# A fused attention and SwiGLU block: 14 of its 22 gate/up products by one level of Strassen's scheme

## The chip, the core and the metric

The kernel runs on one core of a Trainium2 chip. That core has a matrix engine (TensorE, PE in the profile; its weight loads are a row of their own, PEld), a vector engine (VectorE, DVE), a scalar engine (ScalarE, ACT), GpSimd (POOL) and a synchronization engine (SyncE, SP) that issues most of the transfers; 16 DMA engines carry them. The metric is the time of one execution on the device, in microseconds, and of several executions the median.

## The reference

One layer of a hybrid block on 512 tokens of width 1024, in float32. Two kinds of attention are followed by a gated merge, an output projection and a SwiGLU feed-forward layer of width 2816 (22 × 128):

```
x  = x + (sigmoid(h Wg_A) * (o_A Wb_A) + sigmoid(h Wg_B) * (o_B Wb_B)) @ W_out
h2 = rmsnorm(x, g_ffn)
ff = silu(h2 @ W_gate) * (h2 @ W_up)          # 1024 -> 2816, twice
x  = x + ff @ W_down                          # 2816 -> 1024
```

Only the second half, from the output projection on, differs between the two kernels in what is computed where.

## The kernel before

Activations lie transposed: 128 features on the partitions, 512 tokens in the columns. A float32 product is made of three passes over fp32r operands. Every operand is split into a high part (a cast on ScalarE, line 86) and a low part, operand minus high part (a subtraction on VectorE, line 87), and `mm3` (lines 204 to 206) issues high × high, high weight × low activation, low weight × high activation into one PSUM bank:

```
nc.tensor.matmul(out=ps, lhsT=wh, rhs=ah, start=first, stop=False)
nc.tensor.matmul(out=ps, lhsT=wh, rhs=al, start=False, stop=False)
nc.tensor.matmul(out=ps, lhsT=wl, rhs=ah, start=False, stop=last)
```

Weights come as blocks of 128x1024 float32 (512 KB) through `Stream`: SP loads `AHEAD` = 5 blocks ahead into six buffers (`raw`), and the high and low parts of a block (`wh`, `wl`) are made two blocks ahead of their use, in four buffers. A scheduler puts the instructions of each engine in order by their dependencies and their order in the program.

The stages, in the span of the profiled execution: projections and the first attention to about 193 us, the second attention, interleaved with gate projections, to 320, the merge to 343.5, the output projection to 387.3. There x after the first residual (`x2`, eight tiles) is made, and from it `h2` = x2 × g_ffn as high and low parts (`h2h`, `h2l`); the norm of each token, `r2`, is made on the side and applied to products.

Then follow the 22 gate/up pairs. Pair n computes 128 features of gate (`pg`) and 128 of up (`pu`), each over 8 tiles of h2, so 2 × 8 × 3 = 48 matmuls of 512 columns (lines 204 to 206), every one with its own 128x128 weights. VectorE multiplies each with r2 (lines 726 and 728, tiles `t`), ScalarE applies silu to the first (line 727), GpSimd multiplies the two (line 729), and the product is split into `fh`, `fl` for the down projection.

The down projection has eight blocks of 22 × 3 matmuls of 512 columns; each ends with one addition of x2 on VectorE (line 740) and a store, the last block in two halves of 256 columns:

```
parts = 2 if d == 7 else 1
for i in range(parts):
    sl = slice(i * S // parts, (i + 1) * S // parts)
    nc.vector.tensor_tensor(out=x2[d][:, sl], in0=ps[:, sl], in1=x2[d][:, sl], op=ALU.add)
```

Far ahead of all this, in the first attention's `qk_norm` (line 300), GpSimd multiplies the normalized q and k (tiles `qn`) with a gain; that is its first work after it has built the identity matrix `ident`.

Of the kernel before, what the change touches and what calls it, by code (L numbers as in the profile page):

```python
# [9 lines left out]
F32 = mybir.dt.float32  # L10
# [5 lines left out]
P = 128  # L16
# [11 lines left out]
N_BLK, N_RAW, N_SPLIT = 66, 6, 4  # L28
DA_ROUNDS, DA_STAGGER, DA_LEAD = 31, 7, 6
SB_ROUNDS, SB_STAGGER = 36, 4  # L30

# [11 lines left out]
def block_kernel(  # L43
# [22 lines left out]
    small = ctx.enter_context(tc.tile_pool(name="small", bufs=4))  # L66
# [27 lines left out]
    class Stream:  # L94
        AHEAD, SPLIT = 5, 2

        def __init__(self, srcs):
            self.srcs, self.raw, self.hl, self.at = srcs, {}, {}, 0

        def load(self, i):  # L100
            if i < len(self.srcs) and i not in self.raw:
                src = self.srcs[i]
                n = src.shape[-1]
                t = wraw.tile([P, 1024], F32, tag="raw", name=f"raw{i}")
                self.raw[i] = (t, n)
                if i >= KT // 2:
                    nc.sync.dma_start(out=t[:, :n], in_=src)
# [22 lines left out]
        def next(self):  # L130
            i = self.at
            self.at += 1
            if i >= KT // 2:
                for j in range(i, i + self.SPLIT):
                    self.split(j)
# [19 lines left out]
    for n in range(NF):  # L155
        srcs += [w_fg[n], w_fu[n]]
    for d in range(8):
        srcs += [w_dn[d, :, 0:1024], w_dn[d, :, 1024:2048], w_dn[d, :, 2048:2816]]

    ws = Stream(srcs)  # L160
# [66 lines left out]
    def proj_ct(ps, acts, first=True, last=True):  # L227
        wh, wl = ws.next()
# [465 lines left out]

    x2, h2 = [], []
    acc = None
    for d in range(8):
# [3 lines left out]
        nc.vector.tensor_tensor(out=xr, in0=ps, in1=xr, op=ALU.add)  # L701
        x2.append(xr)
# [11 lines left out]

    r2 = B(name="r2")
    ff = []
    for n in range(NF):
# [6 lines left out]
        pu = full_ct(h2)  # L724
        t1, t2 = B(name="t1"), B(name="t2")
        nc.vector.tensor_tensor(out=t1, in0=pg, in1=r2, op=ALU.mult)
        nc.scalar.activation(out=t1, in_=t1, func=AF.Silu)
        nc.vector.tensor_tensor(out=t2, in0=pu, in1=r2, op=ALU.mult)  # L728
        nc.gpsimd.tensor_tensor(out=t1, in0=t1, in1=t2, op=ALU.mult)  # L729
        h, l = B(F32R, "fh"), B(F32R, "fl")  # L730
        split(h, l, t1)
        ff.append((h, l))
    for d in range(8):
        ps = full_ct(ff[0:8], last=False)
        full_ct(ff[8:16], ps=ps, first=False, last=False)
        full_ct(ff[16:22], ps=ps, first=False, last=True)
        parts = 2 if d == 7 else 1
        for i in range(parts):
            sl = slice(i * S // parts, (i + 1) * S // parts)
            nc.vector.tensor_tensor(out=x2[d][:, sl], in0=ps[:, sl], in1=x2[d][:, sl], op=ALU.add)  # L740
            (nc.sync, nc.scalar)[i].dma_start(out=out[d * P : (d + 1) * P, sl], in_=x2[d][:, sl])
# [62 lines left out]
```

## Time and profile before

| | |
|---|---|
| three runs | 751.82, 753.04, 753.18 us; median 753.04 |
| profiled execution, span | 751.0 us |
| TensorE matmul busy | 738.1 us, 98%, 3406 matmuls |
| VectorE busy | 431.8 us, 57% |
| ScalarE busy | 325.1 us, 43% |
| GpSimd busy | 103.0 us, 14% |
| DMA | 71.1 MB, mean 95 GB/s |
| gate/up stage | 387.3 to 627.4 us |
| down projection | 627.4 to 747.5 us |

The span is the time from the first to the last thing that the profile of one execution shows; the runs are timed from outside and hold a little more. An engine's busy time is the union of its instructions. The start of a matmul and the start of the next tell what one costs; its own length (390 ns for 512 columns) holds the pipeline's latency and overlaps with its neighbours. "Idle before" in a row is the time that the engine stood still ahead of an instruction, and what is named behind it is what ended that. A row of the windows view names a stretch and its length, then for PE, PEld, DVE, ACT and POOL the busy time with the count of instructions, then the granted clock of TensorE as a share of full speed, the DMA engines' busy share and GB/s. A row of a timeline has start, duration, engine, line, operation, output <- inputs, shapes and count. A row of groups has busy time in all, mean of one in ns, and the idle time ahead.

### The profile page before, as it was taken

How to read it: one execution, taken by the hardware profiler on the slowest of the kernel's cores; microseconds unless marked ns; L12 is line 12 of the kernel's file. 1: busy time of each engine (PE TensorE's matmuls, PEld its weight loads, DVE VectorE, ACT ScalarE, POOL GpSimd, SP SyncE). 2: the span in 40 equal slices, each digit the busy share in tenths (PEclk: the TensorE clock that was granted, in tenths of full speed). 3: DMA queues.
4: the chain of work that ended last, by engine and by line, in shares of the span. 5: the costliest groups of instructions: out<-in, count | busy, mean ns of one | idle time of the engine just before them, and what ended most of it. 6: DMA issues, size and time to landing. Idle time of an engine off the chain costs nothing.

```text
span 751.0 us, 9018 instructions
## 1 busy us (share of the span) xinstructions
PE 738.1 (98%) x3406; PEld 611.6 (81%) x3406; DVE 431.8 (57%) x648; ACT 325.1 (43%) x514; POOL 103.0 (14%) x139
## 2 busy tenths in 40 slices
PE   8999999999989999999999999999999999999998
PEld 6887887888878878888888888888888888888886
DVE  5856877766687887987446454445545533232220
ACT  6633566877566676544444232323232222222110
POOL 0067000000023223300321011101101111000000
PEclk9999999999999999999999999999999999999999
DMA  8622121211121111244432322332232323333200
GB/s 316 218 98 84 59 83 56 81 61 58 57 84 43 46 39 42 73 152 170 161 120 84 113 84 93 105 103 94 85 112 86 98 83 105 103 118 117 64 14 29
DMA packets 23803, 71.12 MB, mean 95 GB/s; under 512 B 2768, under 2 KB 3408, under 8 KB 23760
## 3 DMA queue, kind: packets, MB, share of 16 engines
q1 hardware_dynamic: 23472, 70.40, 28.0%
q8 instruction: 27, 0.44, 0.2%
q10 hardware_dynamic: 288, 0.15, 0.1%
q14 instruction: 16, 0.13, 0.1%
HBM read 68.44 MB, written 2.10 MB: 94 GB/s over the span
## 4 chain that ended last, share of the span: by engine, by line
PE 89%; DVE 3%; POOL 3%; ACT 2%; issue 2%; DMA 0%; DVEq 0%; POOLq 0%; ACTq 0%
PE pc L204 24%; PE pc L205 24%; PE pc L206 24%; PE pt L221 6%; PE pk L221 3%; PE sc L395 1%; PE sc L394 1%; POOL qn L300 1%; DVE wl L87 1%; PE tb L400 1%; ACT wh L86 1%; PE ta L400 1%; PE av L555 1%; POOL qn L314 1%; PE av L556 1%
## 5 line engine op out<-in xcount | busy, mean ns | idle before, releaser
L86 ACT CAST wh<-raw 128x1024 fp32r<-128x1024 f32 (+2 forms) x136 | 130.9, 963 | 299.1 <-PE pc L205 165.4
L87 DVE TENSOR_TENSOR wl<-raw,wh 128x1024 fp32r<-128x1024 f32 (+2 forms) x136 | 172.7, 1270 | 105.3 <-ACT wh L86 101.2
L204 PE MATMUL pc<-h2h,wh 128*128 128x512 f32 x352 | 137.3, 390 | 0.0
L206 PE MATMUL pc<-h2h,wl 128*128 128x512 f32 x352 | 137.0, 389 | 0.0
L205 PE MATMUL pc<-h2l,wh 128*128 128x512 f32 x352 | 136.9, 389 | 0.0
L204 PE MATMUL pc<-hh,wh 128*128 128x512 f32 x192 | 76.6, 399 | 1.9 <-DVE vs L363 1.5
L205 PEld LDWEIGHTS pc<-h2l,wh 128*128 128x128 f32 x352 | 66.1, 188 | 14.1 <-issue 0.2
L204 PEld LDWEIGHTS pc<-h2h,wh 128*128 128x128 f32 x352 | 66.1, 188 | 14.0 <-issue 0.2
L206 PEld LDWEIGHTS pc<-h2h,wl 128*128 128x128 f32 x352 | 66.1, 188 | 13.5
L206 PE MATMUL pc<-hh,wl 128*128 128x512 f32 x192 | 75.5, 393 | 0.0
L205 PE MATMUL pc<-hl,wh 128*128 128x512 f32 x192 | 75.3, 392 | 0.0
L204 PE MATMUL pc<-fh,wh 128*128 128x512 f32 x176 | 68.5, 389 | 0.0
L205 PE MATMUL pc<-fl,wh 128*128 128x512 f32 x176 | 68.5, 389 | 0.0
L206 PE MATMUL pc<-fh,wl 128*128 128x512 f32 x176 | 68.5, 389 | 0.0
L729 POOL TENSOR_TENSOR t<-t,t 128x512 f32<-128x512 f32 x22 | 30.0, 1363 | 208.5 <-DVE t L728 121.0
L728 DVE TENSOR_TENSOR t<-pc,r 128x512 f32<-128x512 f32 x22 | 15.2, 691 | 67.0 <-PE pc L206 63.2
L204 PEld LDWEIGHTS pc<-hh,wh 128*128 128x128 f32 x192 | 36.4, 190 | 9.2 <-issue 1.7
L206 PEld LDWEIGHTS pc<-hh,wl 128*128 128x128 f32 x192 | 36.2, 189 | 7.8
L205 PEld LDWEIGHTS pc<-hl,wh 128*128 128x128 f32 x192 | 36.4, 190 | 6.7
L530 POOL TENSOR_SCALAR_AFFINE_SELECT om<-om 128x128 f32<-128x128 f32 x32 | 11.4, 356 | 210.4 <-DVE obl L87 138.3
L204 PEld LDWEIGHTS pc<-fh,wh 128*128 128x128 f32 x176 | 33.0, 188 | 6.9
L206 PEld LDWEIGHTS pc<-fh,wl 128*128 128x128 f32 x176 | 33.0, 188 | 6.9
(204 smaller groups left out, 1166.4 us busy)
## 6 DMA issues: line engine op xcount, KB each, us to landing
raw<-w_fg_dram SPq DMA_DIRECT2D x22, 512.0 KB, 3.2
raw<-w_fu_dram SPq DMA_DIRECT2D x22, 512.0 KB, 3.2
raw<-w_gate_dram SPq DMA_DIRECT2D x16, 512.0 KB, 3.2
raw<-w_dn_dram SPq DMA_DIRECT2D x16, 512.0 KB, 3.5
raw<-w_tc_dram SPq DMA_DIRECT2D x12, 512.0 KB, 4.5
raw<-w_ct_dram SPq DMA_DIRECT2D x8, 512.0 KB, 3.3
raw<-w_br_dram SPq DMA_DIRECT2D x16, 256.0 KB, 2.6
raw<-w_out_dram SPq DMA_DIRECT2D x8, 512.0 KB, 3.3
```

The costliest lines, as they stand in the source:

```text
L86: a = nc.scalar.copy(out=h, in_=src)
L87: b = nc.vector.tensor_tensor(out=l, in0=src, in1=f(h), op=ALU.subtract)
L204: nc.tensor.matmul(out=ps, lhsT=wh, rhs=ah, start=first, stop=False)
L205: nc.tensor.matmul(out=ps, lhsT=wh, rhs=al, start=False, stop=False)
L206: nc.tensor.matmul(out=ps, lhsT=wl, rhs=ah, start=False, stop=last)
L221: nc.tensor.matmul(out=pss[tb], lhsT=hx[:, tb * P : (tb + 1) * P], rhs=wx[:, wsl], start=(kt == 0 and i == 0), stop=(kt == KT - 1 and i == 2),
L300: nc.gpsimd.tensor_tensor(out=q3, in0=q3, in1=gqkt[:, gi : gi + 1, :].broadcast_to([P, 8, 64]), op=ALU.mult,)
L314: nc.gpsimd.tensor_tensor(out=q3[:, :, 0:16], in0=t1, in1=t2, op=ALU.add)
L400: nc.tensor.transpose(out=ps[:, off + (tb - sb) * P : off + (tb - sb + 1) * P], in_=tiles[tb][:, sb * P : (sb + 1) * P], identity=ident,)
L530: nc.gpsimd.affine_select(out=t[:, o + w - P : o + w], in_=t[:, o + w - P : o + w], pattern=[[-1, P]], compare_op=ALU.is_gt, fill=fill, ba ...
L728: nc.vector.tensor_tensor(out=t2, in0=pu, in1=r2, op=ALU.mult)
L729: nc.gpsimd.tensor_tensor(out=t1, in0=t1, in1=t2, op=ALU.mult)
```

## The change

Of the 22 pairs, 14 (S in `KINDS`) are computed by one level of Strassen's scheme. For such a pair the weights are a 2 × 2 matrix of blocks (gate and up columns, by the lower and upper half of the 1024 inputs), and the activations one of 2 × 2 blocks as well (lower and upper half of the inputs, lower and upper half of the tokens). Seven products of blocks take the place of eight. One product is 4 input tiles × 3 passes = 12 matmuls of 256 columns; a pair has 84. In the form used there are operand sums on both sides.

- Activation sums, `s13` and `s24`, are made once, in plain pairs 1 and 2 (`operand_sums`), from x2 scaled in place by g_ffn. x2 itself is therefore stored to a scratch tensor in DRAM (`x2d`) when it is made, and read back (`xo`) in the down projection.
- Weight sums are made per pair. T1 and T3 (tile `t13`, 128x1024) are two plain loads by SP and one accumulating DMA issued by GpSimd, which adds the third block to both halves. T2 and T4 (`tb2`, `tb4`) are sums on VectorE. x (`rx`), t13, the pair of T2 and T4 (`wlv`, `whv`) and `b21` are each split into a high and a low part: 3.5 blocks of 128x1024, against 2 of a plain pair.
- The seven products (M1, M3, M5, M7, M6, M4, M2 in this order) are combined on VectorE: three operations of 256 columns and two of 512 for gate (`uu`, `t1`) and two of 256 for up (`t2`).
- r2 is applied to gate ahead of silu as before; for up it is left out, and the product of the pair, now on VectorE, is not scaled by it. The output of the down projection is multiplied by r2 instead (`yo`), and the split of the product is made only in the last three plain pairs and ahead of the down projection.
- The plain pairs are 0 to 2, 8, 14 and 19 to 21. From pair 3 on the order on TensorE, VectorE and ScalarE is that of the program text (`manual_schedule`), not the scheduler's. Raw buffers go from six to five, blocks loaded ahead from five to four, `small` buffers from four to three.

```diff
+KINDS = "PPP" + "SSSSSPSSSSSPSSSS" + "PPP"
...
+        def load_t(self):
+            n = self.n
+            self.t13 = tsum.tile([P, 2 * S], F32, tag="t13", name=f"t13_{n}")
+            nc.sync.dma_start(out=self.t13[:, lo_w], in_=w_fu[n, :, lo_w])
+            nc.sync.dma_start(out=self.t13[:, hi_w], in_=w_fg[n, :, hi_w])
+            nc.gpsimd.dma_start(
+                out=self.t13.rearrange("p (a b) -> p a b", b=S),
+                in_=w_fg[n, :, lo_w].unsqueeze(1).broadcast_to([P, 2, S]), accum_op=ALU.add,
+            )
...
+        def sums(self):
+            self.t2, self.t4 = B(name="tb2"), B(name="tb4")
+            tt(self.t2, self.t13[:, lo_w], self.x[:, hi_w])
+            tt(self.t4, self.t2, self.b21)
...
+        def steps(self):
...
+            self.product(6)
+            tt(uu[:, lo_t], m[6], pe[:, lo_t])
+            tt(uu[:, hi_t], m[7], uu[:, lo_t])
+            two = lambda a: a.rearrange("p (a b) -> p a b", b=half)
+            tt(two(self.t1), m[5].unsqueeze(1).broadcast_to([P, 2, half]), two(uu))
+            tt(self.t1[:, lo_t], m[3], self.t1[:, lo_t])
+            tt(self.t1, self.t1, r2, ALU.mult)
+            self.scale = -1.0
+            self.product(4)
+            self.product(2)
...
+        def tail(self):
+            tt(self.t2[:, hi_t], self.m[4], self.uu[:, hi_t])
+            tt(self.t2[:, lo_t], self.m[2], self.pe[:, lo_t])
+
+        def mul(self):
+            tt(self.t1, self.t1, self.t2, ALU.mult)
+            ff.append(self.t1)
...
+        nc.sync.dma_start(out=x2d[d], in_=xr)
...
+    with tc.manual_schedule(engines={ET.PE, ET.DVE, ET.Activation}):
+        for n in range(N_FIRST, NF):
+            call(n + 2, "load")
+            call(n + 3, "load_t")
+            if prev:
+                prev.silu()
+                prev.tail()
+            steps = pairs[n].steps()
+            next(steps)
+            call(n + 1, "low_a")
+            if prev:
+                prev.mul()
+            call(n + 1, "sums")
+            next(steps)
+            call(n + 1, "prep_b")
+            next(steps)
+            call(n + 1, "prep_c")
...
+            next(steps)
+            call(n + 2, "cast_a")
...
+            yo = B(name="yo")
+            nc.vector.tensor_tensor(out=yo[:, sl], in0=ps[:, sl], in1=r2[:, sl], op=ALU.mult)
+            nc.vector.tensor_tensor(out=xr[:, sl], in0=yo[:, sl], in1=xr[:, sl], op=ALU.add)
```

On VectorE a plain pair of before holds five operations: the r2 products of gate and up (L726, L728; their results are t1 and t2), the low parts of two weight blocks (wl) and that of the pair's result (fl). One pair, in mid-stage:

```order
L728 TENSOR_TENSOR t2563_3943<-pc561_3911,r2552_3803 128x512
L87 TENSOR_TENSOR wl71_4026<-raw71_3885,wh71_4025 128x1024
L87 TENSOR_TENSOR fl565_3949<-t1562_3942,fh564_3948 128x512
L726 TENSOR_TENSOR t1568_4014<-pc566_3952,r2552_3803 128x512
L87 TENSOR_TENSOR wl72_4057<-raw72_3916,wh72_4056 128x1024
```

In the changed kernel the same engine holds, in pair 4 with the preparation of pair 5, the low parts of t, b21 and v (wlt, bl, wlv), the evacuation of M6, M7, M5 and M3 (uu, t1), the factor r2, the tail for up (t2), and then the low part of pair 6's x:

```order
L703 TENSOR_TENSOR wlt5_4298<-t13_5_4036,wht5_4297 128x1024
L703 TENSOR_TENSOR bl619_4301<-b21593_4119,bh618_4300 128x512
L703 TENSOR_TENSOR wlv5_4332<-tb2615_4280,whv5_4331 128x512
L703 TENSOR_TENSOR wlv5_4332<-tb4616_4281,whv5_4331 128x512
L703 TENSOR_TENSOR uu612_4274<-pq622_4337,pe611_4273 128x256
L703 TENSOR_TENSOR uu612_4274<-pc621_4318,uu612_4274 128x256
L703 TENSOR_TENSOR t1613_4275<-pc620_4305,uu612_4274 128x512
L703 TENSOR_TENSOR t1613_4275<-pc617_4284,t1613_4275 128x256
L703 TENSOR_TENSOR t1613_4275<-t1613_4275,r2568_3828 128x512
L703 TENSOR_TENSOR t2614_4276<-pq623_4355,uu612_4274 128x256
L703 TENSOR_TENSOR t2614_4276<-pq624_4368,pe611_4273 128x256
L703 TENSOR_TENSOR wlx6_4382<-rx6_4248,whx6_4381 128x1024
```

The pair's product and the two sums T2 and T4 follow. The evacuation stands behind the low parts of v, which wait for ScalarE's casts of T2 and T4.

On TensorE, in the same place, matmuls of 512 columns that all read one accumulating bank (pc584) for eight input tiles stood before:

```order
L204 MATMUL pc584_4168<-h2h524_3591,wh74_4128 128x512
L205 MATMUL pc584_4168<-h2l525_3592,wh74_4128 128x512
L206 MATMUL pc584_4168<-h2h524_3591,wl74_4129 128x512
L204 MATMUL pc584_4168<-h2h529_3632,wh74_4128 128x512
L205 MATMUL pc584_4168<-h2l530_3633,wh74_4128 128x512
```

Now a bank (pc610, M1 of pair 4) takes four input tiles of half the tokens, and M3 follows in another bank (pc617) with the sums s24 as activations:

```order
L207 MATMUL pc610_4260<-h2h529_3637,whx4_4110 128x256
L208 MATMUL pc610_4260<-h2l530_3638,whx4_4110 128x256
L209 MATMUL pc610_4260<-h2h529_3637,wlx4_4111 128x256
L207 MATMUL pc617_4284<-s24h560_3820,whx4_4110 128x256
L208 MATMUL pc617_4284<-s24l561_3821,whx4_4110 128x256
```

The order of these 84 is M1, M3, M5, M7, M6, M4, M2, and ahead of the gate/up pairs TensorE's order is as it was.

On GpSimd, at the program's start, the products of `qk_norm` followed at once behind the identity matrix:

```order
masks.py:199 AFFINE_SELECT ident_121<-ident_121 128x128
L300 TENSOR_TENSOR qn43_342<-qn43_342,gqkt_106 128x512
L306 TENSOR_TENSOR t100_345<-qn43_342,trigt_108 128x128
L310 TENSOR_TENSOR t200_346<-qn43_342,trigt_108 128x8x8 x2
L300 TENSOR_TENSOR qn44_352<-qn44_352,gqkt_106 128x512
```

Now the accumulating DMAs of the first three Strassen pairs stand there; each waits for SP's two plain loads into its t13:

```order
masks.py:199 AFFINE_SELECT ident_124<-ident_124 128x128
L790 DMA t13_3_3864<-w_fg_dram 128x2x512
L790 DMA t13_4_3937<-w_fg_dram 128x2x512
L790 DMA t13_5_4036<-w_fg_dram 128x2x512
L303 TENSOR_TENSOR qn43_343<-qn43_343,gqkt_109 128x512
```

The scheduler moved these three there, and their six plain loads to SP's first rows, since nothing holds their buffers back.

## Rows read from the trace of the kernel before

**Rows 1.** Head of the page: span, engines' busy time, granted clock by slice.

```profile
span 751.0 us, 9018 instructions
...
PE 738.1 (98%) x3406; PEld 611.6 (81%) x3406; DVE 431.8 (57%) x648; ACT 325.1 (43%) x514; POOL 103.0 (14%) x139
...
PEclk9999999999999999999999999999999999999999
```

**Rows 2.** Windows: pair 0, pairs 1 to 21, down projection; busy time per engine.

```profile
387.30:398.16 10.86, 10.86 (x47) 8.63 (x46) 6.14 (x5) 5.21 (x6) 1.78 (x1) 1.00 0.28 99
398.16:627.40 229.24, 229.24 (x1013) 189.81 (x1012) 113.90 (x107) 69.70 (x85) 28.69 (x21) 1.00 0.29 95
627.40:747.50 120.10, 120.00 (x530) 99.04 (x528) 30.75 (x32) 21.78 (x23) 1.29 (x1) 1.00 0.24 76
```

**Rows 3.** Timeline of TensorE, pair 0's gate: start, duration; first and last of 24.

```profile
387.29 0.39 PE L204 MATMUL pc<-h2h,wh 128*128 128x512 f32 x1
...
392.50 0.40 PE L206 MATMUL pc<-h2h,wl 128*128 128x512 f32 x1
```

**Rows 4.** Timeline of TensorE in the first attention: four of 256 columns, the next.

```profile
87.06 0.28 PE L394 MATMUL sc<-skh,sq 128*128 128x256 f32 x1
...
87.42 0.28 PE L395 MATMUL sc<-skl,sq 128*128 128x256 f32 x1
87.54 0.40 PE L204 MATMUL pc<-hh,wh 128*128 128x512 f32 x1
```

**Rows 5.** Timeline of TensorE, three matmuls of 256 columns behind narrower ones.

```profile
102.33 0.34 PE L204 MATMUL av<-tc,vh 128*128 128x256 f32 x1
102.50 0.28 PE L205 MATMUL av<-tc,vh 128*128 128x256 f32 x1
102.62 0.28 PE L206 MATMUL av<-tc,vl 128*128 128x256 f32 x1
102.74 1.09 PE L221 MATMUL pt<-wh,hh 128*128 128x512 f32 x4
```

**Rows 6.** Timeline of VectorE in the merge, operations back to back.

```profile
341.92 0.68 DVE L689 TENSOR_TENSOR gt<-gt,pc 128x512 f32<-128x512 f32 x1
342.52 1.21 DVE L87 TENSOR_TENSOR wl<-raw,wh 128x1024 fp32r<-128x1024 f32 x1
343.65 0.68 DVE L87 TENSOR_TENSOR ml<-gt,mh 128x512 fp32r<-128x512 f32 x1
```

**Rows 7.** Timeline of VectorE over one plain pair.

```profile
411.06 2.30 DVE L87 TENSOR_TENSOR wl<-raw,wh 128x1024 fp32r<-128x1024 f32 x1 [0.21 <-ACT wh L86]
...
415.60 0.69 DVE L726 TENSOR_TENSOR t<-pc,r 128x512 f32<-128x512 f32 x1 [1.64 <-PE pc L206]
416.50 1.23 DVE L87 TENSOR_TENSOR wl<-raw,wh 128x1024 fp32r<-128x1024 f32 x1 [0.21 <-ACT wh L86]
```

**Rows 8.** Timeline of GpSimd in the same pair.

```profile
411.00 1.29 POOL L729 TENSOR_TENSOR t<-t,t 128x512 f32<-128x512 f32 x1 [7.54 <-DVE t L728]
```

**Rows 9.** ScalarE: timeline of the same pair; groups by shape, casts of 256 columns.

```profile
415.42 1.05 ACT L86 CAST wh<-raw 128x1024 fp32r<-128x1024 f32 x1 [2.48 <-PE pc L205]
416.38 0.62 ACT L727 ACTIVATE t<-t 128x512 f32<-128x512 f32 x1
...
L86 ACT CAST tc<-tc 128x256 fp32r<-128x256 f32 x12 | 4.5, 376 | 4.5 <-PE tc L400 4.5
```

**Rows 10.** The end: timeline of VectorE, and its group by shape.

```profile
747.44 0.76 DVE L740 TENSOR_TENSOR xr<-pc,xr 128x256 f32<-128x256 f32 x2 [14.27 <-PE pc L206]
...
L740 DVE TENSOR_TENSOR xr<-pc,xr 128x256 f32<-128x256 f32 x2 | 0.8, 418 | 14.3 <-PE pc L206 14.3
```

**Rows 11.** DMA issues: count, KB each, median us from issue to landing.

```profile
raw<-w_fg_dram SPq DMA_DIRECT2D x22, 512.0 KB, 3.2
...
xr<-xT_dram SPq DMA_DIRECT2D x8, 256.0 KB, 3.5
```

**Rows 12.** Timeline of GpSimd, the first product of qk_norm.

```profile
37.11 1.29 POOL L300 TENSOR_TENSOR qn<-qn,gqkt 128x512 f32<-128x512 f32 x1 [35.74 <-DVE qn L296]
```

More of the change, by code (lines that the diff above doesn't have):

```diff
@@ L132, in next @@
             self.at += 1
-            if i >= KT // 2:
+            if i >= self.own:
                 for j in range(i, i + self.SPLIT):
@@ L154, in block_kernel @@
     srcs += [w_out[d] for d in range(8)]
-    for n in range(NF):
+    for n in range(N_FIRST):
         srcs += [w_fg[n], w_fu[n]]
-    for d in range(8):
-        srcs += [w_dn[d, :, 0:1024], w_dn[d, :, 1024:2048], w_dn[d, :, 2048:2816]]
-    ws = Stream(srcs)
+    wd = Stream(
+        [w_dn[d, :, a:b] for d in range(8) for a, b in ((0, 1024), (1024, 2048), (2048, 2816))]
+    )
+    ws = Stream(srcs, own=KT // 2)
     xts = []
@@ L225, in proj_tc, with proj_ct @@
             yield
-    def proj_ct(ps, acts, first=True, last=True):
-        wh, wl = ws.next()
+    def proj_ct(ps, acts, first=True, last=True, stream=None):
+        wh, wl = (stream or ws).next()
         n = len(acts)
@@ L695, in block_kernel, with call @@
+    pairs = [(Strassen if k == "S" else Plain)(n) for n, k in enumerate(KINDS)] + [None] * 4
+    def call(n, what):
+        if n < NF:
+            getattr(pairs[n], what)()
+    x2d = nc.dram_tensor("x2_scratch", (KT, P, S), F32, kind="Internal").ap()
     x2, h2 = [], []
@@ new lines, in block_kernel, with split_ff @@
+        if n == 1:
+            operand_sums(1)
+        if n == 2:
+            operand_sums(3)
+            for what in ("sums", "prep_b", "prep_c"):
+                call(N_FIRST, what)
+            call(N_FIRST + 1, "cast_a")
+        nc.vector.tensor_tensor(out=t1, in0=pu, in1=t1, op=ALU.mult)
+        ff.append(t1)
+    fs = []
+    def split_ff():
+        t = ff[len(fs)]
+        h, l = B(F32R, "fh"), B(F32R, "fl")
+        split(h, l, t)
+        fs.append((h, l))
+    ET = mybir.EngineType
@@ new lines, in block_kernel @@
+    last = max(n for n in range(NF) if KINDS[n] == "S")
+    prev = None
+    with tc.manual_schedule(engines={ET.PE, ET.DVE, ET.Activation}):
[15 more added lines that the diff above has]
+            call(n + 1, "prep_c")
+            if n > last:
+                for j in range(3):
+                    wd.load((n - last - 1) * 2 + j)
+                for _ in range(6):
+                    split_ff()
+            if n == NF - 1:
+                wd.split(0)
+            next(steps)
+            call(n + 2, "cast_a")
+            prev = pairs[n]
+        prev.silu()
+        prev.tail()
+        prev.mul()
@@ L737, in block_kernel @@
+    while len(fs) < NF:
+        split_ff()
+    for d in range(8):
+        xr = B(name="xo")
+        nc.sync.dma_start(out=xr, in_=x2d[d])
+        ps = full_ct(fs[0:8], last=False, stream=wd)
+        full_ct(fs[8:16], ps=ps, first=False, last=False, stream=wd)
+        full_ct(fs[16:22], ps=ps, first=False, last=True, stream=wd)
         parts = 2 if d == 7 else 1
```

174 lines of the change are left out of this document (156 added, 18 removed).

## The prediction

> **What bounds the kernel now.** I read the head of the page first, for the busy shares and the granted clock, and then the same engines stage by stage. TensorE is busy 98% of the span and its clock is granted in full, the upper of the two levels, in every slice [rows 1]. In the gate/up stage (pair 0 is the first row of [rows 2], pairs 1 to 21 the second) and in the down projection TensorE is busy in every microsecond, while VectorE is busy in half of the gate/up stage and ScalarE in a third. Nothing waits there that TensorE waits for, so a gain must come out of TensorE's own work, and the question is what becomes of the other engines when it does. One matmul of 512 columns takes its turn every (392.50 − 387.29) / 23 = 0.2265 us [rows 3]. A plain pair has 2 × 8 × 3 = 48 of them: 10.87 us. 21 such pairs are 228.3 us, the second row of [rows 2] with 229.24 to within its edges. The profiled execution is known by its span of 751.0 us; the median of the three runs is 2.0 above it, and I carry that difference over unchanged.
>
> **TensorE's own work.** A Strassen pair has seven products of 4 × 3 matmuls, 84 with 256 columns in place of 48 with 512, that is, of 42 in columns. Every one still loads its own 128x128 weights. Whether a matmul of half the columns takes half the time is the term on which all hangs. The trace of before has the shape: at 87.06 four matmuls of 256 columns, each with other weights, start 0.12 us after one another and the next instruction 0.12 after the last, 0.48 us for four [rows 4]. In the group at 102.33 the second and third are 0.12 apart as well, and the first takes 0.17, behind two of 128 columns [rows 5]. I take 0.120. A pair then costs 84 × 0.120 = 10.08 us, 0.79 less than a plain one, and 14 pairs give **−11.1 us** (0.795 unrounded). Bounds: if the stream held half of [rows 3], 0.1133, a pair would be 9.51 and the 14 would give −19.0. If all went like the whole group at 102.33 (0.41 / 3 = 0.137) a pair would be 11.48 and the 14 would add 8.5. I stay with 0.120, since four in a row hold it and in the other group the excess falls on one matmul. The break-even is 10.87 / 84 = 0.1294. The other eight pairs keep their 48 matmuls, and TensorE's order ahead of the gate/up stage is unchanged row by row.
>
> The Trainium skill ("TensorE: Matmul & The Clock Gate", Back-to-back issue gap) has a warm matmul cost its columns at 2.4 GHz and 2.5 ns on top, which makes 0.109 us of 256 columns. The row of 0.12 speaks against it, and so does the one of 512 columns (0.2265 [rows 3] against its 0.216). By that rule on both sides a pair would save 48 × 0.216 − 84 × 0.109 = 1.2 us and the kernel would come out near 736.9 (an estimate from that page).
>
> **VectorE** is where the change puts its costs. Back to back, an operation on 128x1024 takes 1.13 us until the next may start, one on 128x512 0.60 [rows 6], one on 128x256 0.34 (two of 0.42 in 0.76) [rows 10]. Where an operation reads what the one before wrote, it starts at the end of that, some 0.1 later (its own 0.68 against the 0.60). A Strassen pair has two of 1024 (low parts of x and t), eight of 512 (two sums, three low parts, t1 with M5, t1 with r2, the product) and five of 256 (three in the evacuation, two in the tail), and five of them hang on the one before: 2 × 1.13 + 8 × 0.60 + 5 × 0.34 + 5 × 0.1 = **9.3 us**, in 10.08 of TensorE. Before, a pair had 2.30 + 1.23 + 3 × 0.69, some 5.6 [rows 7]. So VectorE goes from half to 92% and hides with 0.75 us per pair to spare. The average isn't enough, so I follow one pair, in us from its first matmul. The tail of the pair before starts at 0.2 to 0.4; tail, low x, product, two sums, low t and low b21 are 5.5 us, to 5.9. The two low parts of v wait for ScalarE's casts, whose buffer is that of this pair's t, free when product 7 is done at 4 × 1.44 = 5.76: cast until 6.6, low parts until 7.8. Product 6 is done at 7.2, so the five evacuation operations run from 7.8 to 10.4, and the next tail starts 0.3 into the next pair, as assumed: it repeats. TensorE needs from this only the banks back: M3's, freed at 9.9, is wanted by product 3 of the next pair at 11.5, 1.6 us later. VectorE may lag so far without cost, and a plain pair (3.8 us of its own, about 7 with the next pair's preparation, in 10.87) lets it catch up. Cost on the path: 0. Without the cover each us of VectorE beyond 10.08 would cost one per pair once the 1.6 are used up.
>
> A gain lies hidden there too: a low part of 1024 takes 2.30 us beside POOL's product of 1.29 and 1.23 without it [rows 7, 8]. POOL's product goes away, so both low parts cost the short time. The Trainium skill ("SBUF — State Buffer", Who interferes with whom) names the cause: a VectorE operation with two SBUF inputs contends with a GpSimd one that reads SBUF, not with one that only writes. By that rule the accumulating DMA's descriptors, which GpSimd writes, would not bring the 1.07 us back; no run here shows it yet.
>
> **ScalarE** has per Strassen pair two casts of 1.05, four operations of 0.62 (b21, v twice, silu) and one of 0.38: 5.0 of 10.08 [rows 7, 9]. Hidden.
>
> **The start of the Strassen pairs.** In plain pair 2 VectorE gets two operand sums, low x and much of pair 3's preparation, about 10.2 us of 10.87. The last of s24 is due at 420.5 by that count, and product 3 of pair 3 wants it at 420.94 + 1.44 = 422.4. The late evacuation of pair 3 (about 429.7) frees M3's bank at 431.7, wanted at 432.5. Both hold, the second by 0.8. I put 0 on it, 1 us as the upper end.
>
> **Transfers.** A Strassen pair loads 1.25 MB by SP and adds 0.5 MB by POOL, against 1.0 MB. At 0.29 of the DMA engines' time in the second row of [rows 2] that comes to about 0.5. T1 and T3 of pair n + 3 can start when VectorE has read those of pair n, in the middle of pair n − 1, and are wanted in the middle of pair n + 2: some 27 us, less 4 for the two plain loads (3.2 to land [rows 11]): 22 us for the accumulation, which no row shows. Between 3.2 (a plain load of that size) and 13 (four times that) it is hidden. On SP the moved loads and the stores of x2 stand in one queue: the x of block d + 1 now stands behind the store of block d, which waits for d's addition, some 1.0 behind its last matmul. With 3.5 to land [rows 11] and the issue of both it comes some 5 after that matmul, when 24 × 0.2265 = 5.44 later it is wanted; a few tenths more would delay an addition. The last part of h2 is wanted by matmul 21 of pair 0, 4.8 into it, and its addition, cast and low part take 2.2 to 2.5, so 2 us are left. On POOL the first three accumulations stand at the program's start, ahead of qk_norm's products. Those start at 37.11 after 35.74 of idling [rows 12]; I expect the additions issued by about 31. Cost 0, 2 us at most.
>
> **The end.** The down projection hides 8 more products with r2. The last tile ends with four operations of 128x256 for two: 3 × 0.34 + 0.42 against 0.76 [rows 10], **+0.7**.
>
> **Sum**: 751.0 − 11.1 + 0.7 = 740.6, and with the 2.0 carried over **742.6 us**, 10.4 below the median.
>
> **Rivals.**
> (a) Shorter matmuls in full: the 0.12 is the cost of changing from one width to another and dies out in a long stream. Half of [rows 3] then holds, 751.0 − 19.0 + 0.7 + 2.0 = 734.7, if VectorE follows: 9.3 in 9.51, just so. For it: 0.1133 is exactly half. Against: the fourth in a row is no faster than the first [rows 4]. The Trainium skill's rule quoted above is nearest to this side.
> (b) VectorE drags in part: operations that read PSUM, a broadcast or a waiting semaphore cost 0.1 more each. Fifteen of them make 10.8, 0.7 beyond the pair, and after the 1.6 us of lag in each group of five or four some 1 to 2 us per group are lost: 743 to 749.
> (c) Slower: POOL blocks VectorE. Each pair's accumulation is prepared on POOL while VectorE runs two-input operations nearly without gap. One such encounter costs 1.07 [rows 7, 8]; three per pair cost 3.2, VectorE 12.5. A Strassen pair then costs 12.5 instead of 10.87: 14 × 1.6 = 23, less 3 × 1.6 of lag: 753.0 + 18 + 0.7 = 772. It loses from 10.9 us of VectorE per pair, that is from 1.6 extra, half as much as three encounters. For it: VectorE has 8% left. Against: nothing here needs POOL to read SBUF by itself.
> (d) The change doesn't do what it says: 256 columns cost 0.1294 or more, the weight loads being the bound. At 0.1294 the time is 753.7, at 0.137 762. Against: [rows 4].
>
> **How the numbers follow.** Chances: the forecast 0.57; (a) 0.15; (b) 0.11; (c) 0.11, late transfers among it; (d) 0.06, half of it within the range around no change. A measurement of this kernel can tell 0.2%, 1.5 us, from no change. Faster 0.57 + 0.15 + 0.11 + 0.01 = 0.84; same 0.03; slower 0.13. The range runs from (a), 734.5, to the upper end of (b), 749.0; what it leaves out is (c), (d) and some time below (a).
>
> **What would show it.** In the Strassen pairs, matmuls of 256 columns 0.120 us apart and 10.1 us per pair; VectorE about 9.3 us busy per pair, waiting for ScalarE's cast of v; its sums waiting for no DMA; the low part of t near 1.22; the gate/up stage 229.0 us, down from 10.86 + 229.24, with no gap of TensorE at a product 3. The forecast is wrong if the spacing is 0.113 or above 0.125, or if TensorE waits for VectorE at the banks.

## The result, and the profile after

The changed kernel takes 743.57 us (median; 741.73 to 744.94) against 753.08 for the kernel before: a ratio of 0.9883 with a 95% interval of 0.9861 to 0.9904, 9.5 us less. The forecast was 742.6. The profiled execution took 744.94 us, its span is 743.2; its 1.7 us around the span answer to the 2.0 that the forecast carried over.

The head of the page of the changed kernel, to be read against [rows 1]:

```profile
span 743.2 us, 10437 instructions
...
PE 729.6 (98%) x3910; PEld 628.1 (85%) x3910; DVE 502.4 (68%) x835; ACT 362.8 (49%) x586; POOL 87.9 (12%) x131
```

TensorE still works 98% of the span, with fewer microseconds of work in more instructions. VectorE has gone up by 71 us. The stages are read from TensorE's timeline. These are, in the changed kernel, the first matmul of the first Strassen pair, the first of the next pair, the first of the down projection and the kernel's last:

```profile
423.58 0.28 PE L207 MATMUL pc<-h2h,whx 128*128 128x256 f32 x1
...
433.65 0.28 PE L207 MATMUL pc<-h2h,whx 128*128 128x256 f32 x1
...
619.16 0.39 PE L207 MATMUL pc<-fh,wh 128*128 128x512 f32 x1
...
738.61 0.39 PE L209 MATMUL pc<-fh,wl 128*128 128x512 f32 x1
```

In the kernel before, the last two of these stand at

```profile
627.56 0.39 PE L204 MATMUL pc<-fh,wh 128*128 128x512 f32 x1
...
747.01 0.39 PE L206 MATMUL pc<-fh,wl 128*128 128x512 f32 x1
```

One Strassen pair is (433.65 − 423.58) / 84 = 0.1199 us per matmul. The windows of the changed kernel (columns as in [rows 2]) show the first five Strassen pairs, one of them (pair 6), the gate/up stage, and the down projection to the start of its last matmul:

```profile
423.58:473.97 50.39, 50.39 (x421) 50.39 (x420) 45.49 (x74) 23.83 (x35) 6.00 (x5) 1.00 0.78 203
...
453.81:463.89 10.08, 10.08 (x86) 10.08 (x85) 9.29 (x16) 4.76 (x7) 1.19 (x1) 1.00 0.79 169
...
390.03:619.20 229.17, 229.17 (x1564) 213.60 (x1563) 186.17 (x289) 108.44 (x159) 15.14 (x13) 1.00 0.50 136
619.20:738.61 119.41, 119.41 (x528) 98.88 (x527) 34.30 (x37) 21.15 (x22) 0.00 (x0) 1.00 0.33 102
```

In all of these TensorE is busy in every microsecond. From its own first matmul to the first of the down projection the gate/up stage has 619.16 − 390.03 = 229.13 us, where it had 627.56 − 387.29 [rows 3] = 240.27: 11.1 less. (The edges of [rows 2] cut 0.2 off that stage.) The down projection is as long as it was, 738.61 − 619.16 = 747.01 − 627.56 = 119.45. The end behind the last matmul starts at 738.61 and lasts 4.6 us, 0.6 more than before (751.0 − 747.0 = 4.0). These three make 751.0 − 11.1 + 0.6 = 740.5. But the gate/up stage begins at 390.03 and not at 387.29 [rows 3]. The 2.7 us were lost at the very start, as the timelines of TensorE's first projection show, of the kernel before

```profile
5.78 1.19 PE L221 MATMUL pt<-wh,hh 128*128 128x512 f32 x4 [0.78 <-ACT wh L86]
6.81 1.08 PE L221 MATMUL pt<-wh,hl 128*128 128x512 f32 x4
```

and of the changed one:

```profile
6.26 2.07 PE L224 MATMUL pt<-wh,hh 128*128 128x512 f32 x4 [0.93 <-ACT wh L89]
8.13 1.91 PE L224 MATMUL pt<-wh,hl 128*128 128x512 f32 x4
9.84 1.69 PE L224 MATMUL pt<-wl,hh 128*128 128x512 f32 x4
11.37 1.08 PE L224 MATMUL pt<-wh,hh 128*128 128x512 f32 x4
```

Twelve matmuls (four per row) take 11.37 − 6.26 = 5.11 us, 0.43 each, the pace of the lower clock level, where four of the kernel before take 1.03. From the thirteenth on they go at 0.227 here too. The trace agrees on when that changed: its record of the granted clock begins at 11.15 us, at the upper level, and that of the kernel before at 4.54. The clock rose late in this execution. The first one comes 0.48 later as well, since its weights are cast later. The other executions of the changed kernel have spans of 743.0, 740.7 and 740.0. The executions of the kernel before that stood beside the experiments have spans from 749.1 to 753.5. So a spread of this kind is not the change's; the last section returns to it.

### The profile page after: what moved, and what is told of

It is laid out like the page before. It is cut to its first block, busy times and chain, and to the rows that moved or that the text cites. A ratio compares the mean times of both kernels' runs of the same rounds, so it can differ in the third digit from the quotient of the medians.

```text
span 743.2 us, 10437 instructions
## 1 busy us (share of the span) xinstructions
PE 729.6 (98%) x3910; PEld 628.1 (85%) x3910; DVE 502.4 (68%) x835; ACT 362.8 (49%) x586; POOL 87.9 (12%) x131
## 3 DMA queue, kind: packets, MB, share of 16 engines
q1 hardware_dynamic: 31824, 78.26, 32.6%
q0 software_dynamic: 3808, 7.34, 5.7%
## 4 chain that ended last, share of the span: by engine, by line
PE 87%; DVE 4%; POOL 3%; ACT 3%; issue 2%; DMA 1%; DVEq 0%; POOLq 0%; ACTq 0%
PE pc L207 20%; PE pc L208 20%; PE pc L209 20%; PE pt L224 6%; PE pq L208 4%; PE pq L207 4%; PE pq L209 4%; PE pk L224 3%; PE sc L398 1%; PE sc L397 1%; DVE wl L90 1%; ACT wh L89 1%; POOL qn L303 1%; PE ta L403 1%; DMA colt<-cols_dram 1%
## 5 line engine op out<-in xcount | busy, mean ns | idle before, releaser
L89 ACT CAST wh<-raw 128x1024 fp32r<-128x1024 f32 (+2 forms) x98 | 90.8, 929 | 167.7 <-PE pc L208 121.1
L90 DVE TENSOR_TENSOR wl<-raw,wh 128x1024 fp32r<-128x1024 f32 (+2 forms) x98 | 106.0, 1081 | 97.0 <-ACT wh L89 84.9
L208 PEld LDWEIGHTS pc<-fl,wh 128*128 128x128 f32 x176 | 33.0, 188 | 6.9
L790 POOL DMA_DIRECT2D t<-w_fg_dram x14 | 16.9, 1209 | 166.7 <-DMA t<-w_fg_dram 70.9
L207 PE MATMUL pc<-s13h,wht 128*128 128x256 f32 x112 | 31.7, 283 | 0.0
L208 PE MATMUL pc<-s13l,wht 128*128 128x256 f32 x112 | 31.7, 283 | 0.0
L209 PE MATMUL pc<-s13h,wlt 128*128 128x256 f32 x112 | 31.7, 283 | 0.0
L537 DVE TENSOR_TENSOR_SCAN cu<-om 128x512 f32<-128x512 f32 (+3 forms) x32 | 27.0, 844 | 4.4 <-POOL om L533 4.3
L224 PE MATMUL pt<-wh,hh 128*128 128x512 f32 x96 | 27.8, 406 | 0.9 <-ACT wh L89 0.9
L721 ACT CAST whx<-rx 128x1024 fp32r<-128x1024 f32 x14 | 14.7, 1049 | 26.1 <-issue 22.5
```

What stands on the lines that cost most here:

```text
L89: a = nc.scalar.copy(out=h, in_=src)
L90: b = nc.vector.tensor_tensor(out=l, in0=src, in1=f(h), op=ALU.subtract)
L224: nc.tensor.matmul(out=pss[tb], lhsT=hx[:, tb * P : (tb + 1) * P], rhs=wx[:, wsl], start=(kt == 0 and i == 0), stop=(kt == KT - 1 and i == 2),
L537: nc.vector.tensor_tensor_scan(out=cum[:, sl][:, ::-1], data0=om[:, sl][:, ::-1], data1=om[:, sl][:, ::-1], initial=1.0, op0=ALU.mult, op1 ...
L721: nc.scalar.copy(out=hl[0], in_=src)
L790: nc.gpsimd.dma_start(out=self.t13.rearrange("p (a b) -> p a b", b=S), in_=w_fg[n, :, lo_w].unsqueeze(1).broadcast_to([P, 2, S]), accum_op ...
```

## The experiments

Each kernel is the changed one with one edit, and two combine two.

**All pairs plain.**

```diff
-KINDS = "PPP" + "SSSSSPSSSSSPSSSS" + "PPP"
+KINDS = "P" * 22
```

> All 22 pairs plain, and everything else of the changed kernel kept (x2 stored and read back, r2 at the down projection's output, hand order, five raw buffers); the operand sums go. Theory: the gain is TensorE's alone, 14 x 0.79 = 11.1 us, so it is lost here: 743.6 + 11.1 = 754.7, between 753 and 756, with matmuls of 512 columns 0.227 us apart and no gap. Rival: the new structure around the pairs (no product on GpSimd, r2 once less per pair) brought a part of the gain: below 750.

Measured: 754.73 us (752.99 to 756.53), 1.0027 of the kernel before (1.0012 to 1.0041). The difference to the changed kernel is 11.2 us. So the whole gain is that of the 14 pairs, and what was built around them costs about 1.5 us by itself. Of that, 0.6 is the end; in its trace three gaps of TensorE behind the first product of pair 0 hold some 0.35 more than the two of the kernel before (what ends them the trace does not name). The remainder, some 0.5, is less than the spread of its executions (spans of 751.0 to 754.5).

**Sixteen in a row, and eighteen.**

```diff
-KINDS = "PPP" + "SSSSSPSSSSSPSSSS" + "PPP"
+KINDS = "PPP" + "S" * 16 + "PPP"
```

> Pairs 3 to 18 all by Strassen's scheme, no plain pair between them. Theory: VectorE needs 9.3 us of 10.08 per pair, so it needs no plain pair to catch up: two more pairs save 2 x 0.79 = 1.6 us, 742.0 (741 to 743.3), no gap of TensorE. Rival: VectorE is at 9.7 to 10 us per pair and falls behind without the plain pairs, TensorE waits at product 3's bank: 744 or more.

Measured: 739.52 us (738.93 to 740.78), 0.9825 of the kernel before (0.9807 to 0.9844). One window over all sixteen pairs, and one over pair 14:

```profile
420.97:582.24 161.27, 161.27 (x1346) 161.27 (x1344) 147.66 (x239) 76.31 (x112) 15.59 (x13) 1.00 0.64 167
531.90:541.98 10.08, 10.08 (x86) 10.08 (x86) 9.29 (x16) 4.77 (x7) 1.20 (x1) 1.00 0.73 202
```

161.27 / 1344 = 0.1200: no gap in sixteen pairs, and VectorE stands at 9.29 in 10.08 in the twelfth of them as in the fourth. The plain pairs between are not needed for VectorE to catch up. In the trace the two pairs bring the 1.6 us expected; the median lies 2.5 lower than expected. In the profiled execution that is the start: its gate/up stage begins at 387.41, 2.6 earlier than in the changed kernel's. Of the other four there is no trace (spans of 737.2 to 739.1 in all).

With `"S" * 18 + "P"` behind the first three pairs:

> Pairs 3 to 20 by Strassen's scheme, one plain pair at the end; the splits for the down projection that stood in three plain pairs now stand in the last one and ahead of the down projection. Theory: two more pairs save 2 x 0.79 from sixteen's 739.5: 737.9, TensorE without gap. Rival: the down projection waits for the low parts of the products (14 tiles at 0.60 on VectorE against 0.68 per tile on TensorE, with weights to split beside them): a gap behind the last pair and 739 or more.

Measured: 739.98 us (738.49 to 740.72), 0.982 of the kernel before (0.9801 to 0.9839). From the first gate matmul to the last one of the kernel its trace has 1.6 us less than that of sixteen, as expected, and no gap ahead of the down projection. The medians don't show it: its executions differ by up to 2.2 us (spans of 736.8 to 739.0). Sixteen and eighteen are both faster than the changed kernel and can't be told from each other by these times.

**The sums T1 and T3 on VectorE.**

```diff
-            nc.gpsimd.dma_start(
-                out=self.t13.rearrange("p (a b) -> p a b", b=S),
-                in_=w_fg[n, :, lo_w].unsqueeze(1).broadcast_to([P, 2, S]), accum_op=ALU.add,
-            )
+            self.b11 = B(name="b11")
+            nc.sync.dma_start(out=self.b11, in_=w_fg[n, :, lo_w])
...
+            for sl in (lo_w, hi_w):
+                tt(self.t13[:, sl], self.t13[:, sl], self.b11)
```

> T1 and T3 by two additions of 512 on VectorE from a third plain load, no accumulating DMA. Theory: VectorE then needs 9.3 + 2 x 0.60 = 10.5 us of 10.08 and falls 0.4 behind per pair; after the 1.6 us of lag that the banks allow TensorE waits, at the end of each group of Strassen pairs: 744 to 748, gaps at product 3. Rivals: the lag is free over five pairs (743.6 within 1), or each pair pays in full (14 x 0.4 = 6 us, 749 or more).

Measured: 743.58 us (743.02 to 745.63), as the changed kernel. The time alone would speak for the first rival. Its profiled execution, with a span of 743.9, had no late clock at the start, though, and TensorE's waits in gate/up (engine and line, for what: total, times, longest) are

```profile
PE pc L207 <- DVE uu L703: 1.4, 4, 0.7
```

four times at product 3, once in each of pairs 4 to 7, 2.5 us in all as the spacing of the matmuls tells. In the groups of pairs 9 to 13 and 15 to 18 there is none. VectorE enters the first group behind and the others with slack, and there five pairs use no more of it than the banks allow (the section on the prediction has the rows). Whether the first group's loss is the price of VectorE over its limit, or a start effect, was left to the same edit in sixteen in a row:

> Pairs 3 to 18 by Strassen's scheme without a plain one between, and T1 and T3 by two additions on VectorE in place of the accumulating DMA. With plain pairs between, the sums on VectorE cost 2.5 us, all in the first group (pairs 3 to 7), at 0.49 per pair, so VectorE needs 10.57 per pair. Theory: without plain pairs that price is paid in all pairs, some 15 x 0.49 + 0.5 = 7.9 more than sixteen in a row with the DMA: 739.5 + 7.9 = 747.4, slower than with fourteen. Rival: the loss is a start effect of the first group and stays 2.5: 742.

Measured: 750.45 us (746.77 to 751.15), 10.9 more than sixteen with the accumulating DMA, and 3.0 more than the theory had. The trace shows the 7.9 of the theory, in the sixteen pairs. The other executions have no trace (spans of 745.1 to 749.4); the two of them with a mean granted clock of 0.999 have 745.1 and 745.2, 7.3 to 8.0 above the three of sixteen in a row at 1.000 (737.2 to 737.8). What the median has beyond that stays open. The waits, and TensorE's and VectorE's rows around one of them (the VectorE rows at 443.67 and 444.86 read M7 and M3 of the pair that has just ended):

```profile
PE pc L207 <- DVE uu L703: 4.1, 15, 0.7
...
444.15 0.39 PE L207 MATMUL pc<-s24h,whx 128*128 128x256 f32 x1 [0.24 <-DVE uu L703]
...
443.67 0.42 DVE L703 TENSOR_TENSOR uu<-pc,uu 128x256 f32<-128x256 f32 x1
444.86 0.42 DVE L703 TENSOR_TENSOR t<-pc,t 128x256 f32<-128x256 f32 x1
...
454.25 0.42 DVE L703 TENSOR_TENSOR uu<-pc,uu 128x256 f32<-128x256 f32 x1
```

VectorE's round from `uu` to `uu` is 454.25 − 443.67 = 10.58 us, and so is TensorE's: the kernel is bound by VectorE from the second Strassen pair on. Product 3 of the next pair starts at 444.15, when `uu` has been made from M7 (443.67 + 0.42), and not when M3 has been read, which is the row at 444.86 and still to come. So the bank that it waits for is M7's. The row gives a wait of 0.24 us; by the starts of the matmuls it costs 0.50, since the two spacings around it are 0.52 and 0.22 instead of 0.12. That is the price of 1.2 us more on VectorE where no plain pair stands between: 0.5 us per pair, and the accumulating DMA is what keeps it away.

**The first sums held back.**

```diff
+            if n < N_FIRST + 3:
+                nc.vector.tensor_copy(out=self.t13[:, S - 1 : S + 1], in_=gA[7][:, 0:2])
```

> The T1 and T3 loads and accumulations of the first three Strassen pairs can't start until the merge is done (a copy of two columns from the merge's last tile into each t13 holds them back), so that nothing of them stands at the program's start. Spans of the changed kernel fall near 740 or near 743, and in the profiled one the first twelve matmuls are 0.43 us apart, not 0.227. Theory: that comes from when the first tiles land and when TensorE's clock rises, and not from the moved transfers, which stand behind the first loads: both kinds of span again, median within 1.5 of 743.6. Rival: the moved transfers delay the first tiles: all spans near 740, times 741 to 742.5, first matmul of the projection at 5.8 us. A second rival: the late sums make product 5 of pair 3 wait: a gap of TensorE of over 1 us there.

Measured: 749.91 us (746.73 to 752.2), 0.9952 of the kernel before (0.9935 to 0.997): 6.3 us slower than the changed kernel, and the theory on the time fell. On the start it held as far as traces go: here the first projection begins at 5.43 us, and with the transfers at the program's start it begins at 5.33 in the trace of the product back on GpSimd and at 5.27 in that of the widths (both below), so they need not delay it. The loss is none of the outcomes that were named. GpSimd's accumulations, VectorE's additions of x (blocks 2 and 7), TensorE's longest wait in pair 0, and a window that begins within that wait:

```profile
353.12 2.58 POOL L792 DMA_DIRECT2D t<-w_fg_dram  x2 [36.12 <-DVE xr L895]
...
369.72 0.69 DVE L895 TENSOR_TENSOR xr<-pc,xr 128x512 f32<-128x512 f32 x1 [8.45 <-DMA xr<-xT_dram]
...
394.68 0.69 DVE L895 TENSOR_TENSOR xr<-pc,xr 128x512 f32<-128x512 f32 x1 [2.86 <-DMA xr<-xT_dram]
...
396.18 0.80 PE L207 MATMUL pc<-h2h,wh 128*128 128x512 f32 x1 [3.58 <-ACT h2h L900]
...
394.90:401.70 6.80, 5.27 (x9) 2.81 (x10) 3.99 (x5) 4.87 (x6) 1.51 (x1) 0.50 0.38 125
```

The x of block 2 is issued at 358.25 and takes 11.4 us to land, where such a load takes 4.1 in the median of this trace; the DMA engines are full meanwhile (share 1.06 from 356 to 370), with the accumulations and their plain loads among the transfers. Each later x stands in SP's queue behind the store of the block before, so the delay is handed on to the last block, and TensorE waits for h2 in pair 0. There the granted clock falls as well: in the window it is 0.50, and nine matmuls go at the lower level. From the first matmul of pair 0 to the kernel's last the trace has 357.5 us, the changed kernel 348.6: waits and clock together cost 8.9 us. (The late clock of the changed kernel's start, 2.7, and its lower clock in the second attention are absent in this execution, so the spans differ by less.) At the start of the program the same transfers cost nothing that a trace shows.

**The product back on GpSimd.**

```diff
-            tt(self.t1, self.t1, self.t2, ALU.mult)
+            nc.gpsimd.tensor_tensor(out=self.t1, in0=self.t1, in1=self.t2, op=ALU.mult)
```

> The product of gate and up in the Strassen pairs goes back from VectorE to GpSimd. VectorE loses 0.60 us per pair and, as in the kernel before, one of its operations on two SBUF inputs that runs beside the product of 1.29 us gets up to 1.07 longer: 9.3 - 0.6 + 1.07 = 9.8 of 10.08. Theory: still hidden, 743 within 1.5 as the changed kernel, and the profile shows one stretched operation in each Strassen pair, where the accumulating DMA's 1.2 us on GpSimd stretched none. Rival: VectorE is pushed over its 10.08 and TensorE waits: 745 or more. Second rival: no operation is stretched, since the 2.30 of the kernel before had another cause: VectorE at 8.7 per pair.

Measured: 742.76 us (741.55 to 744.99), the same as the changed kernel. GpSimd's product, VectorE's sum T2 beside it, and T2's mean over the 14 pairs (groups by shape), first here and then in the changed kernel:

```profile
444.97 2.13 POOL L877 TENSOR_TENSOR t<-t,t 128x512 f32<-128x512 f32 x1
...
445.86 1.79 DVE L703 TENSOR_TENSOR tb<-t,rx 128x512 f32<-128x512 f32 x1
...
L703 DVE TENSOR_TENSOR tb<-t,rx 128x512 f32<-128x512 f32 x14 | 21.7, 1549 | 0.0
```

```profile
L703 DVE TENSOR_TENSOR tb<-t,rx 128x512 f32<-128x512 f32 x14 | 9.5, 681 | 0.0
L703 DVE TENSOR_TENSOR wlt<-t,wht 128x1024 fp32r<-128x1024 f32 x13 | 15.8, 1218 | 0.0
L790 POOL DMA_DIRECT2D t<-w_fg_dram x14 | 16.9, 1209 | 166.7 <-DMA t<-w_fg_dram 70.9 <-DVE t L703 36.0 <-ACT bh L721 33.7
```

A product on GpSimd stretches the VectorE operation beside it from 0.68 to 1.55 on average, as in [rows 7, 8]. VectorE is then busy 9.94 us of the 10.08 of pair 6, a little over the 9.8 expected, and still just keeps up. The 1.2 us that GpSimd spends on an accumulating DMA stretch none: the means of the changed kernel are those of undisturbed operations (0.681, 1.218), and the two T2 and three wlt that ran beside such a DMA took 0.68 and 1.22 like the rest. This agrees with the rule of the Trainium skill ("SBUF — State Buffer", Who interferes with whom) that a VectorE operation with two SBUF inputs contends with a GpSimd one that reads SBUF, not with one that only writes.

**The price of a matmul by its columns.** The edit narrows ten of each product's twelve matmuls:

```diff
+                n = {1: 256, 3: 240, 5: 224, 7: 208, 6: 192, 4: 160, 2: 128}[i]
```

> In the 14 Strassen pairs the inner ten of each product's twelve matmuls have fewer columns: M1 256, M3 240, M5 224, M7 208, M6 192, M4 160, M2 128 (the other tokens are left out of the sums; first and last matmul stay at 256). 256 columns take 0.1200 us and 512 take 0.2267, so a line through both has 13.3 ns and 0.4167 ns per column. Theory: each matmul costs its columns and a fixed 13.3 ns: 240 columns 113, 224 107, 208 100, 192 93, 160 80 ns. Rival: 0.120 is a floor, since every matmul loads its own 128x128 weights: 0.120 at all widths. In between: the line holds down to some floor below 0.120, seen as the spacing at which narrower matmuls stop gaining.

Its one execution took 734.69 us, which is no time of the block, since the kernel leaves tokens out of its sums. The rows of TensorE show a change from 256 to 128 columns, the run of 128, the change back to 256, and the first and last of a run of 224:

```profile
447.89 0.23 PE L845 MATMUL pq<-h2l,bh 128*128 128x128 f32 x1
447.95 0.28 PE L845 MATMUL pq<-h2h,bl 128*128 128x128 f32 x1
...
448.84 0.28 PE L845 MATMUL pq<-h2l,bh 128*128 128x128 f32 x1
448.95 0.33 PE L845 MATMUL pq<-h2h,bl 128*128 128x256 f32 x1
449.12 0.28 PE L845 MATMUL pc<-h2h,whx 128*128 128x256 f32 x1
...
452.14 0.27 PE L845 MATMUL pc<-s13h,wlt 128*128 128x224 f32 x1
...
453.04 0.27 PE L845 MATMUL pc<-s13l,wht 128*128 128x224 f32 x1
```

With 128 columns the spacing is (448.84 − 447.95) / 8 = 0.111 us, with 224 it is 0.90 / 8 = 0.113, and over all the Strassen pairs the median is between 0.111 and 0.112 at every width from 128 to 240. The third outcome, then: the line through 256 and 512 columns ends at a floor of about 0.111, and 256 columns at 0.1200 lie just above it. The changes of width say more: the first matmul of 128 columns behind one of 256 is followed after 0.06 us (447.95 − 447.89), and the first of 256 behind 128 takes 0.17 (449.12 − 448.95), as in [rows 5]. So a narrow matmul is not itself held to 0.111; what is held to it is something that each of them needs and that is done while the one before runs. That this is the weight load, which every one of these matmuls has, is likely, and no run here leaves the loads out. The Trainium skill ("TensorE: Matmul & The Clock Gate", LDWEIGHTS (loading the stationary operand)) has a weight load take its 128 columns at 1.2 GHz, which makes 0.107 us (an estimate from that page) and is near it. The issue gap of the same page that the prediction quoted, 0.109 for 256 columns, is not met in any pair of the changed kernel.

**A longer warm-up.**

```diff
-WARM = 2
+WARM = 3
```

> Eighteen in a row, and three warm-up products of 1.7 us at the program's start where there were two. In the profiled execution of the changed kernel TensorE stood still 0.93 us between the warm-up and the first projection and then ran its first twelve matmuls 0.43 us apart instead of 0.227; in the kernel before it stood still 0.78 us and ran at 0.227 from the second on. Theory: the pause decides; the longer warm-up lasts to 6.7 us, past the landing of the first tiles, costs 0.5 to 0.9 us on good starts and takes the 2.4 us off the bad ones: spans closer together, all between 737.3 and 738.7 but for the 1.7 us that the clock costs in the second attention in some executions. Rival: the late clock has nothing to do with the pause: first matmuls at 0.43 us in some executions still, spans as wide as before (736.8 to 739.0) and 0.5 to 0.9 higher.

Measured: 739.61 us (738.74 to 740.23) against 739.98 without. The spans are 737.0 to 738.5, within 1.5 us where those of eighteen without it were within 2.2. That is in the direction of the theory, but five executions each don't tell it from chance, and the expected cost on good starts isn't seen (737.0 against 736.8). Neither of the two traces, with three warm-up products or with two, has the twelve slow matmuls that the edit was to remove, so they can't show them removed. It stays open.

## Why the prediction was right

- **TensorE's own work.** Forecast −11.1 at 0.120 us per matmul. The stage has 240.27 − 229.13 = 11.1 less, the rows have 0.1199, the 1344 of sixteen in a row 0.1200, and with all pairs plain 11.2 us come back. Four matmuls in a row [rows 4] were enough to read the price; the longer first one of [rows 5] was an effect of the change in width (0.17 again at 448.95 in the widths). Rival (a), that half the columns take half the time, is out: the fixed part of 13.3 ns does not die out in a stream of 1344. Rival (d) is out by the same rows.
- **VectorE.** Forecast 9.3 us in 10.08 and the path through a pair followed by hand. The window of pair 6 has 9.29. Pairs 3 to 5 have 9.98, 9.88 and 9.73: VectorE enters the group behind, as the forecast's section on the start had it, and works that off. The forecast had it waiting for ScalarE's cast of v, and VectorE's waits from the first of the fourteen pairs to the last (for what: total, times, longest) show that, ten times:

```profile
DVE wlv L703 <- ACT whv L721: 5.9, 10, 0.6
```

Its other waits there stand where a group of Strassen pairs begins or ends, and cost TensorE nothing, which is busy in every microsecond. Rival (b), 0.1 more per operation, did not come; that 1.2 us more is too much without plain pairs between was shown with the sums on VectorE. Rival (c), GpSimd's preparation of the accumulations, was looked for and not found (0.681 and 1.218 above).
- **The lag.** The forecast named the wrong bank. It had product 3 wait for M3's, 1.6 us ahead; the sums on VectorE show that it waits for M7's, which is read two operations earlier. In pair 6 of the changed kernel that read ends at 462.43 and product 3 of the next pair starts at 465.33, so VectorE could lag by 2.9 us more, not 1.6. In pairs 3 and 4, where it is still behind, 1.7 and 2.4 are left. With the sums on VectorE the same distance shrinks by 0.49 a pair: 2.33, 1.84, 1.35 and 0.86 us in pairs 9 to 12, and the plain pair 14 comes before it is used up. The rows are those of pair 6 in the changed kernel, then of pair 12 with the sums on VectorE:

```profile
462.01 0.42 DVE L703 TENSOR_TENSOR uu<-pc,uu 128x256 f32<-128x256 f32 x1
...
465.33 0.28 PE L207 MATMUL pc<-s24h,whx 128*128 128x256 f32 x1
...
525.99 0.42 DVE L703 TENSOR_TENSOR uu<-pc,uu 128x256 f32<-128x256 f32 x1
...
527.27 0.28 PE L207 MATMUL pc<-s24h,whx 128*128 128x256 f32 x1
```

- **Transfers.** Forecast: no cost. That held, with two sizes off. The DMA engines' share is 0.78 in the first five Strassen pairs, and 0.58 from the first of the fourteen to the last, not 0.5. A part of that is that the accumulating queue (q0) takes more of the engines per byte than the plain one (q1). An accumulation takes 7.4 us to land, within the 3.2 to 13 assumed:

```profile
q1 hardware_dynamic: 31824, 78.26, 32.6%
q0 software_dynamic: 3808, 7.34, 5.7%
...
t<-w_fg_dram POOLq DMA_DIRECT2D x14, 512.0 KB, 7.4
```

5.7 / 7.34 is 1.9 times 32.6 / 78.26. And the x behind the stores delays the last additions of the output projection by more than the tenths forecast:

```profile
386.82 0.69 DVE L893 TENSOR_TENSOR xr<-pc,xr 128x512 f32<-128x512 f32 x1 [3.24 <-DMA xr<-xT_dram]
...
391.49 0.69 DVE L893 TENSOR_TENSOR xr<-pc,xr 128x512 f32<-128x512 f32 x1 [2.19 <-DMA xr<-xT_dram]
```

The stage's last matmul starts at 389.80 and lasts 0.39 us; its addition could have run from 390.2 and ran at 391.49. So 1.3 of the 2 us that were said to be left were used, and the first sums held back show what comes when they are all used.
- **The moved accumulations on GpSimd.** Forecast: issued by about 31 us, ahead of the first product of qk_norm. The third is issued at 32.78, and the product still waits for VectorE, as in [rows 12] but less:

```profile
32.78 1.20 POOL L790 DMA_DIRECT2D t<-w_fg_dram  x1 [2.29 <-DMA t<-w_fg_dram]
...
39.77 1.29 POOL L303 TENSOR_TENSOR qn<-qn,gqkt 128x512 f32<-128x512 f32 x1 [5.79 <-DVE qn L299]
```

39.77 − 37.11 is the 2.7 us of the start and nothing more.
- **The clock.** The forecast took it as granted in full in every slice [rows 1]. A 9 in that row stands for 90% or more, and the last section has a window of the kernel before with 0.86. It lies ahead of the gate/up stage and changes no term of the sum.
- **The end.** Forecast +0.7, measured 4.6 − 4.0 = +0.6.

The terms of the change came out to a tenth of a microsecond (740.5 for 740.6) in the profiled execution; the 2.7 us that its start lost are in no term. That the median still lies within 1 us of 742.6 is in part luck: two of the four executions have spans of 740.0 and 740.7 and two of 743, and the median falls between.

## What to carry to other kernels

Where one engine is busy in every microsecond, fewer columns for it are a gain of known size: price the new shape by a run of equal instructions in the trace of before, even a short one, but not by those next to a change of width, and follow one round of the engine that takes over the work, operation by operation, against the new round of the first. Splitting once more would not pay here: below 224 to 240 columns a matmul with new weights costs 0.111 us whatever its width, and a second level would put 49 × 6 / 2 = 147 matmuls of 128 columns into a pair, 16.3 us (an estimate from that spacing). And a step that is taken off a full engine is not free to sit anywhere. 1.2 us more per pair on VectorE cost 7.9 us of the 13.7 that sixteen pairs in a row had gained (2.5 us in the trace with plain pairs between), and the same transfers some 330 us later gave back two thirds of the gain.

## What the runs showed of the hardware

TensorE's time per matmul with its own weights followed two lines: 13.3 ns and 0.4167 ns per column between 256 and 512 columns (0.1200 and 0.2267 us), and a floor of 0.111 below.

A narrow matmul directly behind a wide one was not held to that floor (0.06 us at 128 columns), and the wide one behind a narrow one paid for it (0.17 at 256).

Apart from pair 0 with the first sums held back, TensorE's clock was at the lower level in two places, and not in every execution. At the start the record of the granted clock begins, at the upper level, at 11.15 us in the trace of the changed kernel and between 4.5 and 7.3 us in the ten others. Ahead of that the column of the windows reads 1.00 for want of a record. The twelve matmuls at 0.43 us, 2.4 us lost, are the ones ahead of this late rise. The pause in front of them, 0.93 us, is the longest of the eleven traces (0.78 in the kernel before, none to 0.78 in the others), but with one such trace no run tells whether the pause has to do with it.

In the second attention TensorE waits 2.35 to 2.37 us for VectorE in all eleven traces. These are the windows around it, in the kernel before and in eighteen in a row:

```profile
214.00:226.00 12.00, 9.64 (x43) 7.89 (x42) 9.28 (x15) 7.34 (x14) 2.17 (x4) 0.86 0.24 87
```

```profile
214.00:226.00 12.00, 9.63 (x50) 7.87 (x49) 10.13 (x17) 8.08 (x16) 2.48 (x5) 1.00 0.27 87
```

The same pause and the same busy time, but 43 matmuls at a granted clock of 0.86 against 50 at 1.00; the stretch around it took some 1.6 us more (seven matmuls). Eight of the eleven traces have the lower clock behind this wait; the three without are eighteen in a row, with either warm-up, and the first sums held back. The executions without a trace fit: of the twelve with all pairs plain, the four with a mean granted clock of 1.000 have spans of 751.0 to 751.3, the eight with 0.997 or 0.998 752.3 to 754.5. No run here settles what decides between the two outcomes, nor how much of the spread comes from the start.
